# Scaling and rotating each half of the tokens in a quantum of its own, with transposes and scores one quantum later, in the attention layer of a two-layer trunk

## The chip, the core and the metric

The kernel runs on one core of a Trainium2 chip. The metric is device time in microseconds of one execution. The engines are named as in the profile: PE is the matrix engine (PEld its weight loads), DVE the vector engine, ACT the scalar engine, POOL the engine called GpSimd, SP the engine that issues most of the loads. Each engine takes its own instructions in order; between engines there are semaphores.

## What is computed

A trunk of two layers on 256 tokens of 2048 features, all in float32. Layer 0 mixes tokens by block-sparse attention; with 256 tokens there is one block of 256 keys, so it is causal attention with 16 heads of 128. Layer 1 mixes by multi-head latent attention. Each is followed by a gated channel mixer with a short convolution. The change lies in layer 0's attention:

```python
def moba_attention(h, pos, wq, wk, wv, gq, gk, wo):
    ...
    q = rope(rms_norm((h @ wq).reshape(B, S, H, dh), gq), pos, rot)   # rot = 32 of 128
    k = rope(rms_norm((h @ wk).reshape(B, S, H, dh), gk), pos, rot)
    v = (h @ wv).reshape(B, S, H, dh)
    ...
    s_own = jnp.einsum('bqhd,bhkd->bhqk', qc, k_own).astype(F32) * scale
    ...
    return o.reshape(B, S, H * dh) @ wo
```

So every head of q and of k is divided by its root mean square, multiplied by a gain, and has its first 32 numbers rotated by the token's position, before the scores.

## The kernel before

**Products in three parts.** Every weight is split into a high part (`whi`, rounded to the matrix engine's fp32r type) and the rest (`wlo`), and so is every activation. A product is three matmuls: high by high, low weight by high, high weight by low. Weights come in *pieces* of 128 x 512 numbers. `Stream.split` makes the two parts of a piece: ACT casts `whi` (line 104), DVE subtracts to get `wlo` (line 105). The buffers for the parts hold five pieces, so the cast for piece n+5 waits until PE has done with piece n.

**Quanta.** PE's work is a list of quanta, one for each piece, 192 of them for q, k and v of layer 0: four groups of four heads, and in each group 16 quanta for q, 16 for k, 16 for v. A quantum there is six matmuls of 512 columns (`tok_major`, line 235), three for each half of 128 tokens. Around the quanta the program is written out in a fixed order by a loop at its end: before quantum q come the parts of all pieces up to q+3 (after the first 18 quanta), then the matmuls of q, then everything that was attached to q by `at(q, ...)`. Nothing reorders this later: every engine meets its instructions in this order, so a DVE instruction attached to quantum q stands behind the `wlo` of piece q+3 and ahead of the `wlo` of piece q+4.

**Heads.** When the 16 quanta of q (or k) of a group are done, `plan_heads` attaches their further work (`q` is the last of these quanta; for the first group q's work starts 15 quanta later and k's 9 later, since it needs the norm of the tokens):

- `evac` (ACT, lines 372 and 374) copies the products out of PSUM, at q.
- `squares` (DVE, line 379) sums the squares of each head, one half of the tokens at q+1, the other at q+2.
- `rstd` at q+3: DVE writes `hms` (line 387), POOL raises it to the power -1/2 into `hr` (line 392).
- `scaled` (DVE, line 405, four instructions for each half) multiplies by `hr` and the gain, in place in `qk`.
- `rotate` (DVE, lines 435, 436, 439 and 440) rotates the first 32 numbers of the four heads of a half.
- `turned` (PE, line 449) transposes two heads at a time, four transposes; `queries_out` or `keys_out` copies them out of PSUM by two ACT copies and one DVE subtraction.

**Scores.** For each head the class `Head` plans scores and the masked row maximum (`biased`, line 495) at its quantum, exponentials one quantum later, division (`normal`) two later, the transpose of the probabilities (`turn`, `turned`) five later, and the product with the values (`values`, `parted`, lines 553 and 554) eight later. The values of a group are copied out (`evac_parts`, lines 608, 609 and 612) at the last quantum of v.

The latent attention of layer 1 calls `plan_heads` too, with `late` at its default of 0 and no rotation there.

Of the kernel before, what the change touches and what calls it, by code (L numbers as in the profile page):

```python
# [115 lines left out]
def trunk(ctx: ExitStack, tc: tile.TileContext, a, out):  # L116
# [99 lines left out]
    def at(q, f, *args):  # L216
        side.setdefault(q, []).append((f, args))

    def first(q, f, *args):
        ahead.setdefault(q, []).append((f, args))  # L220

    def add(f, *args):
        quanta.append((f, args))
        return len(quanta) - 1
# [26 lines left out]
    def feat_major(state, rhs, k0, k_last, first, t_hi, t_lo, n, half=0):  # L251


        if first and half == 0 and "acc" not in state:
            open_bank(state)
        src = rhs()
        o = state["acc"][:, half * S : (half + 1) * S]
        for k in range(n // P):
            kt = k0 + k
            w_hi, w_lo = t_hi[:, k * P : (k + 1) * P], t_lo[:, k * P : (k + 1) * P]  # L260
            mm(o, w_hi, src[:, kt, :S], start=first and k == 0, stop=False, skip_group_check=True)  # L261
            mm(o, w_hi, src[:, kt, S:], start=False, stop=False, skip_group_check=True)  # L262
            mm(o, w_lo, src[:, kt, :S], start=False, stop=kt == k_last, skip_group_check=True)  # L263
# [358 lines left out]
    def plan_heads(q, hs, key, step, out=None, late=0):  # L622

        at(q, hs.evac)
        for t in range(NT):
            at(q + step * (1 + t), hs.squares, t)
        at(q + step * 3, hs.rstd)
        for t in range(NT):
            at(q + step * (5 + t), hs.scaled, t)
            at(q + step * (5 + t), hs.rotate, t)  # L630
        for i0 in (0, 2):
            pair = {}
            q1 = q + step * 9 + i0 // 2 + late
            at(q1, lambda hs=hs, p=pair, i0=i0, key=key: hs.turned(env[key], p, i0))
            if out is None:
                at(q1, lambda hs=hs, p=pair, i0=i0, key=key: hs.turned_out(env[key], p, i0))
            else:
                at(q1, lambda p=pair, i0=i0, key=key: out(env[key], p["tp"], i0))
# [3 lines left out]
    for g in range(4):  # L642
        for kind in "qkv":
            state = {"first": g == 0 and kind == "q"}
            for kt in range(KD):
                q = add(tok_major, state, lambda: n1.h, kt, KD - 1)
                if g == 0 and kind == "q" and kt + 1 < KD:
                    first(q + 1, n1.scaled, kt + 1)
                if g == 0 and kind == "k" and kt < 12:
                    for j in range(kt * 4 // 3, (kt + 1) * 4 // 3):  # L650
                        at(q, n1.square, j)
                        at(q + 1, n1.total, j)
            if g == 0 and kind == "q":
                at(q + 14, n1.sums)
            if kind == "q":
                at(q, moba_tiles, g)
            if kind == "v":
                at(q, evac_parts, state, ("v", g), lambda: n1.rstd)
                q_v = q
            else:  # L660
                hs = Heads(state, 4, P, G_Q if kind == "q" else G_K, 32, (tab, T_MC, T_MS), lambda: n1.rstd)
                plan_heads(q + (0 if g else 15 if kind == "q" else 9), hs, ("qT" if kind == "q" else "kT", g), 1,
                           queries_out if kind == "q" else keys_out, 1)
                q_k = q
        for i in range(4):
            hd = Head(
                4 * g + i, lambda g=g: env["qT", g], lambda g=g: env["kT", g], lambda g=g: env["v", g],
                i, lambda: env["oT"], MOBA_SCALE, parts=True,
            )
            q0 = q_k + (13 if g else 21) + (2 * i if g == 3 else 3 * i)  # L670
            hd.plan(q0, max(q0 + 8, q_v + 3 + i))


# [260 lines left out]
    for r in range(4):  # L934
        state = {}
        for kq in range(4):
            q = add(lambda t_hi, t_lo, n, st=state, kq=kq: feat_major(
                st, lambda: n3.h, 4 * kq, KD - 1, kq == 0, t_hi, t_lo, n))
# [48 lines left out]
    for half in range(2):  # L987
        state = {}
        for kt in range(KD):
            q = add(tok_major, state, lambda: n3.h, kt, KD - 1)  # L990
# [22 lines left out]
    for g in range(4):  # L1013
        if g == 1:
            rotary_queries(1, 2)
        for kind in "kqv" if g else "qkv":
            state = {}
            for kt in range(4):
                q = add(tok_major, state, lambda kind=kind: env["cqT" if kind == "q" else "ckvT"], kt, 3)
            if kind == ("k" if g else "q"):  # L1020
                at(q, mla_tiles, g)
            if kind == "v":
                at(q, evac_values, state, ("v", g), None)
            else:
                q_q = q
                hs = Heads(state, 4, P, None, 0, None, (lambda: cq["scale"]) if kind == "q" else None,
                           C_GQN if kind == "q" else C_GKN)
                plan_heads(q, hs, ("qT" if kind == "q" else "kT", g), 1)
        for i in range(4):
            hd = Head(  # L1030
                4 * g + i, lambda g=g: env["qT", g], lambda g=g: env["kT", g], lambda g=g: env["v", g],
                i, lambda: env["oT"], MLA_SCALE,
                rope=lambda h=4 * g + i: (env["qrT"][:, h // 2, :], env["kr"][h % 2]),
            )
            q0 = q_q + 11 + 3 * i
            hd.plan(q0, q0 + 7)
# [131 lines left out]
```

## Time and profile before

| | us |
|---|---|
| median of three runs | 2099.79 (2099.70 to 2100.92) |
| the profiled execution | 2099.88 |
| its span in the profile | 2098.0 |
| PE busy in the span | 2089.0 |
| DVE busy in the span | 1405.3 |
| ACT busy in the span | 1138.3 |
| granted PE clock, all slices | full |

The span is what the profiler saw from the first to the last instruction; the rest of the execution's time, 1.88 us, lies around it. Matmuls are pipelined and a matmul's record lasts longer than the interval at which the next can start, so PE's busy share says little of small waits: those are read from the distance between the starts of matmuls.

### The profile page before, as it was taken

Reading aid. Unit: us, or ns where it says so; the run is one execution under the profiler, and the core shown is the slowest. Engines: PE = TensorE matmul, PEld = TensorE weight load, DVE = VectorE, ACT = ScalarE, POOL = GpSimd, SP = SyncE. Lnnn points to the kernel's source line nnn. Section 1 sums busy time; section 2 is a strip of 40 time slices with the busy share of each in tenths; the row PEclk is TensorE's granted clock in tenths of the full one; section 3 lists DMA queues with packets and bytes.
Section 4 is the critical chain, followed back from the end, with each engine's and each line's share of the span. In section 5 each row is a group of like instructions: output and inputs, shape, how many; then the busy total and the mean of one; then the engine's idle time right before and its main releaser. Section 6 shows DMA issues by size and latency. Waiting matters only on the chain.

```text
span 2098.0 us, 42200 instructions
## 1 busy us (share of the span) xinstructions
PE 2089.0 (100%) x16716; PEld 2014.2 (96%) x16716; DVE 1405.3 (67%) x3072; ACT 1138.3 (54%) x2238; POOL 45.6 (2%) x37
## 2 busy tenths in 40 slices
PE   9999999999999999999999999999999999999999
PEld 7888889999999999999999889999999999999999
DVE  6776776776666766655556786766766667655554
ACT  6555555655555555545555675655555555544443
POOL 0000000000000000000000110000000000000000
PEclk9999999999999999999999999999999999999999
DMA  7444445555555555555554533555555555555553
GB/s 272 161 170 173 170 171 185 194 188 198 195 190 200 191 191 201 194 190 198 194 191 159 175 139 108 195 181 201 187 196 199 187 199 195 189 205 209 193 207 131
DMA packets 59382, 391.83 MB, mean 187 GB/s; under 512 B 6960, under 2 KB 10032, under 8 KB 13232
## 3 DMA queue, kind: packets, MB, share of 16 engines
q1 hardware_dynamic: 59040, 388.87, 52.3%
q8 instruction: 131, 2.15, 0.4%
q14 instruction: 67, 0.55, 0.1%
q10 hardware_dynamic: 144, 0.26, 0.0%
HBM read 387.01 MB, written 2.10 MB: 185 GB/s over the span
## 4 chain that ended last, share of the span: by engine, by line
PE 96%; DVE 2%; POOL 0%; ACT 0%; issue 0%; DMA 0%; SPq 0%; ACTq 0%; DVEq 0%; POOLq 0%
PE acc L261 26%; PE acc L263 26%; PE acc L262 26%; PE acc L235 15%; PE tp L449 1%; DVE wlo L105 1%; PE sc L489 0%; PE sc L486 0%; PE tp L521 0%; POOL hr L392 0%; DVE junk L379 0%; PE sc L546 0%; DVE qk L405 0%; DMA xT<-in_xT 0%; PE sc L465 0%
## 5 line engine op out<-in xcount | busy, mean ns | idle before, releaser
L105 DVE TENSOR_TENSOR wlo<-raw,whi 128x512 fp32r<-128x512 f32 (+1 forms) x1480 | 1000.1, 684 | 399.0 <-ACT whi L104 396.0
L104 ACT CAST whi<-raw 128x512 fp32r<-128x512 f32 (+1 forms) x1479 | 871.6, 614 | 459.6 <-PE acc L262 212.3
L261 PE MATMUL acc<-h,whi 128*128 128x256 f32 x2880 | 796.1, 276 | 0.0
L263 PE MATMUL acc<-h,wlo 128*128 128x256 f32 x2880 | 795.9, 276 | 0.0
L262 PE MATMUL acc<-h,whi 128*128 128x256 f32 x2880 | 795.8, 276 | 0.0
L261 PEld LDWEIGHTS acc<-h,whi 128*128 128x128 f32 x2880 | 540.9, 188 | 0.0
L263 PEld LDWEIGHTS acc<-h,wlo 128*128 128x128 f32 x2880 | 540.9, 188 | 0.0
L262 PEld LDWEIGHTS acc<-h,whi 128*128 128x128 f32 x2880 | 540.9, 188 | 0.0
L262 PE MATMUL acc<-a,whi 128*128 128x256 f32 x1408 | 389.1, 276 | 0.0
L263 PE MATMUL acc<-a,wlo 128*128 128x256 f32 x1408 | 389.0, 276 | 0.0
L261 PE MATMUL acc<-a,whi 128*128 128x256 f32 x1408 | 389.0, 276 | 0.0
L235 PE MATMUL acc<-whi,h 128*128 128x512 f32 (+1 forms) x896 | 274.6, 381 | 0.0
L263 PEld LDWEIGHTS acc<-a,wlo 128*128 128x128 f32 x1408 | 264.4, 188 | 0.0
L262 PEld LDWEIGHTS acc<-a,whi 128*128 128x128 f32 x1408 | 264.4, 188 | 0.0
L261 PEld LDWEIGHTS acc<-a,whi 128*128 128x128 f32 x1408 | 264.4, 188 | 0.0
L235 PEld LDWEIGHTS acc<-whi,h 128*128 128x128 f32 x896 | 165.0, 188 | 30.0 <-ACT whi L104 0.7
L235 PE MATMUL acc<-wlo,h 128*128 128x512 f32 (+1 forms) x448 | 170.4, 381 | 2.1 <-DVE wlo L105 2.0
L261 PE MATMUL acc<-oT,whi 128*128 128x256 f32 x512 | 144.9, 283 | 0.0
L263 PE MATMUL acc<-oT,wlo 128*128 128x256 f32 x512 | 141.9, 277 | 0.0
L262 PE MATMUL acc<-oT,whi 128*128 128x256 f32 x512 | 141.7, 277 | 0.0
L740 DVE TENSOR_TENSOR g<-acc,rstd_b 128x256 f32<-128x256 f32 x88 | 37.5, 426 | 125.7 <-PE acc L263 122.7
L747 ACT ACTIVATE c<-g,par 128x256 f32<-128x256 f32 x88 | 53.1, 603 | 108.1 <-DVE g L740 108.1
(160 smaller groups left out, 1603.8 us busy)
## 6 DMA issues: line engine op xcount, KB each, us to landing
raw<-in_ffn_gu SPq DMA_DIRECT2D x176, 1024.0 KB, 4.8
raw<-in_ffn_down SPq DMA_DIRECT2D x88, 1024.0 KB, 4.8
raw<-in_moba_wk SPq DMA_DIRECT2D x16, 1024.0 KB, 4.9
raw<-in_moba_wv SPq DMA_DIRECT2D x16, 1024.0 KB, 4.8
raw<-in_moba_wo SPq DMA_DIRECT2D x16, 1024.0 KB, 4.8
raw<-in_mla_wo SPq DMA_DIRECT2D x16, 1024.0 KB, 4.8
raw<-in_moba_wq SPq DMA_DIRECT2D x13, 1024.0 KB, 4.9
raw<-in_mla_wkv_a SPq DMA_DIRECT2D x8, 576.0 KB, 3.7
```

What stands on the lines that cost most here:

```text
L104: self.nc.scalar.copy(hi[:, :n], w)
L105: self.nc.vector.tensor_tensor(lo[:, :n], w, hi[:, :n].bitcast(F32), op=ALU.subtract)
L235: mm(state["acc"][t][:, :n], src[:, kt, c : c + P], (t_lo if part == 1 else t_hi)[:, :n], start=kt == 0 and part == 0, stop=kt == k_last a ...
L261: mm(o, w_hi, src[:, kt, :S], start=first and k == 0, stop=False, skip_group_check=True)
L262: mm(o, w_hi, src[:, kt, S:], start=False, stop=False, skip_group_check=True)
L263: mm(o, w_lo, src[:, kt, :S], start=False, stop=kt == k_last, skip_group_check=True)
L449: nc.tensor.transpose(tp[:, (i * NT + t) * P : (i * NT + t + 1) * P], flat[:, t, c : c + P], ident)
L740: nc.vector.tensor_tensor(self.g[:, 2:], self.gate["acc"][:, :S], self.norm.rstd_b, op=ALU.mult)
L747: nc.scalar.activation(self.c, self.g[:, 2:], AF.Identity, bias=par[:, cb : cb + 1], scale=self.cw(2))
```

## The change

```diff
@@ plan_heads
         for t in range(NT):
-            at(q + step * (5 + t), hs.scaled, t)
-            at(q + step * (5 + t), hs.rotate, t)
+            at(q + step * (5 + t) + late * (1 + t), hs.scaled, t)
+            at(q + step * (5 + t) + late * (2 + t), hs.rotate, t)
         for i0 in (0, 2):
             pair = {}
-            q1 = q + step * 9 + i0 // 2 + late
+            q1 = q + step * 9 + i0 // 2 + 2 * late
...
@@ heads of layer 0
-            q0 = q_k + (13 if g else 21) + (2 * i if g == 3 else 3 * i)
+            q0 = q_k + (14 if g else 22) + (2 * i if g == 3 else 3 * i)
             hd.plan(q0, max(q0 + 8, q_v + 3 + i))
```

In layer 0 (`step` and `late` both 1), the first half is scaled at q+6 and rotated at q+7, where both stood at q+5; the second half is scaled at q+8 and rotated at q+9, where both stood at q+6. The transposes move from q+10 and q+11 to q+11 and q+12. All work of the heads, from the scores to the product with the values, moves one quantum later: in `max(q0 + 8, q_v + 3 + i)` the first term is the larger for every head, before and after. With `late` at 0, as in layer 1, all these numbers stay as they were. No instruction is added or taken away, and the lists of SP and of POOL keep their order.

## The prediction

> **What bounds the kernel now.** I read the page's busy times first, then the groups by line and form, then the stage of layer 0's q, k and v as a window, then the order of time on PE, DVE, ACT and POOL around each small wait.
>
> ```profile
> span 2098.0 us, 42200 instructions
> PE 2089.0 (100%) x16716; PEld 2014.2 (96%) x16716; DVE 1405.3 (67%) x3072; ACT 1138.3 (54%) x2238; POOL 45.6 (2%) x37
> ```
> ```profile
> L235 PE MATMUL acc<-wlo,h 128*128 128x512 f32 x384 | 151.0, 394 | 2.0 <-DVE wlo L105 2.0
> ```
> ```profile
> 11.60:309.20 297.60, 296.10 (x1449) 246.80 (x1449) 221.17 (x658) 173.29 (x384) 16.89 (x9) 1.00 0.52 185
> ```
>
> PE sets the end: 2089.0 of 2098.0 us, at the full granted clock (the 1.00 of the stage's row). A change on DVE can then only pay where PE waits for DVE. In layer 0's products the second row names such waits: 2.0 us ahead of matmuls with `wlo`. A record ends later than its successor can start, so the true price is in the starts. PE's order of time (start, duration):
>
> ```profile
> 62.43 0.39 PE L235 MATMUL acc<-wlo,h 128*128 128x512 f32 x1
> 62.66 0.61 PE L235 MATMUL acc<-whi,h 128*128 128x512 f32 x2
> 63.60 0.50 PE L235 MATMUL acc<-wlo,h 128*128 128x512 f32 x1 [0.33 <-DVE wlo L105]
> 63.94 0.62 PE L235 MATMUL acc<-whi,h 128*128 128x512 f32 x2
> 64.40 0.40 PE L235 MATMUL acc<-wlo,h 128*128 128x512 f32 x1
> ...
> 64.87 0.60 PE L449 MATMUL tp<-ident,qk 128*128 128x128 f32 x4
> ...
> 77.63 0.39 PE L235 MATMUL acc<-wlo,h 128*128 128x512 f32 x1
> ...
> 79.28 0.50 PE L235 MATMUL acc<-wlo,h 128*128 128x512 f32 x1 [0.81 <-DVE wlo L105]
> ...
> 80.08 0.40 PE L235 MATMUL acc<-wlo,h 128*128 128x512 f32 x1
> ...
> 80.55 0.60 PE L449 MATMUL tp<-ident,qk 128*128 128x128 f32 x4
> ...
> 117.03 0.39 PE L235 MATMUL acc<-wlo,h 128*128 128x512 f32 x1
> ...
> 118.23 0.50 PE L235 MATMUL acc<-wlo,h 128*128 128x512 f32 x1 [0.36 <-DVE wlo L105]
> ...
> 119.03 0.40 PE L235 MATMUL acc<-wlo,h 128*128 128x512 f32 x1
> ...
> 119.50 0.60 PE L449 MATMUL tp<-ident,qk 128*128 128x128 f32 x4
> ...
> 140.39 0.39 PE L235 MATMUL acc<-wlo,h 128*128 128x512 f32 x1
> ...
> 141.14 0.50 PE L235 MATMUL acc<-wlo,h 128*128 128x512 f32 x1
> ...
> 287.67 0.39 PE L235 MATMUL acc<-wlo,h 128*128 128x512 f32 x1
> ...
> 288.40 0.50 PE L235 MATMUL acc<-wlo,h 128*128 128x512 f32 x1
> ```
>
> Undisturbed, a `wlo` matmul follows the last by 0.68 us (62.43, and 63.11 expected): three matmuls, half a quantum, so a quantum is 1.36. The reader is to see 63.60 in place of 63.11, and 0.80 instead of 0.68 to the next: 0.61 lost. At 79.28 it is 0.97 + 0.12 = 1.09, at 118.23 it is 0.52 + 0.12 = 0.64. There is one such place for each of the eight sets of heads (q and k of four groups), always a few matmuls ahead of the first transposes of L449. The other five lie from 141.14 to 288.40 and are near misses: 0.75 - 0.68 = 0.07 at the first, 0.05 at the last, and some 0.11 behind each as at the large ones, 0.16 to 0.18 together. Sum over the stage: 0.61 + 1.09 + 0.64 + 5 x 0.17 = 3.2 us. That is all that DVE costs PE there and all that this change can win.
>
> **Why DVE is late at these places.** The chain at the first, on DVE, with POOL and ACT:
>
> ```profile
> 56.08 1.30 DVE L105 TENSOR_TENSOR wlo<-raw,whi 128x512 fp32r<-128x512 f32 x2
> 58.31 1.14 DVE L405 SCALAR_TENSOR_TENSOR qk<-qk,hr,gains 128x128 f32<-128x128 f32 x4 [0.93 <-POOL hr L392]
> 59.48 0.29 DVE L435 TENSOR_TENSOR ro<-qk,tab 128x128 f32<-128x128 f32 x1
> ...
> 60.29 0.69 DVE L105 TENSOR_TENSOR wlo<-raw,whi 128x512 fp32r<-128x512 f32 x1
> 60.89 1.13 DVE L405 SCALAR_TENSOR_TENSOR qk<-qk,hr,gains 128x128 f32<-128x128 f32 x4
> ```
> ```profile
> 56.26 2.02 POOL L392 TENSOR_TENSOR hr<-hms,mhalf 128x8 f32<-128x8 f32 x1 [5.60 <-DVE hms L387]
> ```
> ```profile
> 56.29 0.62 ACT L104 CAST whi<-raw 128x512 fp32r<-128x512 f32 x1 [0.74 <-PE acc L235]
> 57.65 0.62 ACT L104 CAST whi<-raw 128x512 fp32r<-128x512 f32 x1 [0.74 <-PE acc L235]
> ```
>
> DVE stands still for 0.93 us until POOL's powers land, then scales and rotates the first half (58.31 to 60.29: 1.17 and 0.81), makes one `wlo` (0.60 to the next start), does the second half the same way to 62.87, and only then makes the `wlo` that PE wants at 63.11; it is ready some 0.6 later. The cast that this `wlo` needs was done at 57.65 + 0.62 = 58.27. So it lies 4.6 us behind work that no one wants so soon: the first transposes come at 64.87.
>
> **The change part by part.** Nothing is added or removed; POOL's and SP's instructions keep their order, so no load is issued elsewhere. *Scaling and rotating in four quanta.* Behind the two differences at 56.08 now comes a third (its cast is done at 56.29 + 0.62 = 56.91): 57.38 to 58.0, inside the 0.93 us of idleness. Then, by the durations above and 0.62 for a difference (0.60 from 60.29 to 60.89, rounded up): scaling 58.31 to 59.48, the difference that was late before ready at 60.1, rotation to 60.9, a difference to 61.5, second scaling to 62.7, a difference to 63.3, second rotation to 64.1. The difference wanted at 63.11 has 3.0 us to spare; none later has less than two, since a quantum with scaling takes 1.79 and one with rotation 1.43 against PE's 1.36: four of them fall behind by 1.0 in all. All eight waits go: -3.2 us.
>
> *Transposes one quantum later.* Between the last rotation and the first transposes lay four quanta, now two. At the first place the transposes come at 64.87 - 0.61 + 1.36 = 65.6, against 64.1: 1.5 us to spare. The five small places have the same DVE chain with PE less early, so the same or a little more. Two places are tighter, since other work falls among the halves:
>
> ```profile
> 75.54 0.69 ACT L612 ACTIVATE v<-acc,rstd 128x512 f32<-128x512 f32 x1
> 76.13 1.65 ACT L104 CAST whi<-raw 128x512 fp32r<-128x512 f32 x3
> ```
> ```profile
> 113.57 0.37 ACT L553 CAST oT<-sc 128x256 fp32r<-128x256 f32 x1 [2.58 <-PE sc L544]
> 113.84 1.75 ACT L104 CAST whi<-raw 128x512 fp32r<-128x512 f32 x3
> ```
>
> For k of group 0 the values are copied out in the quantum of the first rotation; the cast behind them ends at 76.13 + 0.62 - 0.61 = 76.1, and then follow on DVE a difference, scaling, a difference, rotation: 3.22 us, to 79.4. The transposes come at 80.55 - 0.61 - 1.09 + 1.36 = 80.2: 0.8 to spare. For q of group 1 the last head's product with the values now falls in the quantum of the first rotation and stands ahead of it on DVE. From the cast at 113.57 to the transposes are 119.50 - 0.64 - 113.57 = 5.3 us, the same number of quanta as after the change; DVE needs from there about 0.4 until it can start line 554 (the cast's 0.37), 0.42 for it (its row below), and 0.81 + 0.62 + 1.17 + 0.62 + 0.81: 4.9. 0.4 to spare. I take 0 for waits of the transposes; the bounds are 0 and, if those two are late by as much as they now have in hand, some 1.2.
>
> *Scores and what follows one quantum later.* The same instructions on the same engines, all shifted together, so their own spacing is kept. New company, for group 0: the division of the last head's probabilities, the copy of the third's transposes and the second's values now meet the first squares of group 1's q.
>
> ```profile
> L379 DVE CUSTOM_DVE_ANT_0 junk<-qk 128x128 f32<-128x128 f32 x128 | 29.6, 289 | 0.0
> L554 DVE TENSOR_TENSOR oT<-sc,oT 128x256 fp32r<-128x256 f32 x32 | 13.6, 424 | 24.0 <-ACT oT L553 24.0
> L513 DVE TENSOR_SCALAR s<-s,sst 128x256 f32<-128x256 f32 x32 | 11.1, 348 | 0.0
> L535 DVE TENSOR_TENSOR pT<-tp,pT 128x256 fp32r<-128x256 f32 x16 | 6.8, 424 | 2.3 <-ACT pT L534 1.7
> ```
>
> On DVE that is 4 x 0.289, twice 0.424, and for the division at most twice 0.348: 2.7 us, with a difference 3.3, so it falls 2.0 behind in a quantum of 1.36, and with the second squares 0.4 more. A difference made as soon as its cast is done has 63.11 - (58.27 + 0.69) = 4.1 us of lead. I take 0; if only half the lead were there, it would cost 0.3. In the last group the work ends a quantum deeper in the output projection, which reads these four heads only from its 25th quantum on; the last values come in its 12th. 0.
>
> One rule speaks against the third difference. The Trainium skill, "SBUF — State Buffer", section "Who interferes with whom", says that a DVE instruction with two SBUF inputs and a GpSimd instruction that reads SBUF shut each other out, the second waiting until the first is done. By that rule the third difference would push the powers, or be pushed, by 0.62 us, and take that from the 1.5 us in hand; the sum would stay within 0.1 of mine but the turn would be nearer. The row at 56.08 speaks against it: its second difference, from 56.7 to 57.4, ran at its usual length inside the powers' 56.26 to 58.28.
>
> **The sum.** The profiled execution took 2099.88 us, 2098.0 of span and 1.88 around it. 2099.88 - 3.2 = 2096.7. It lies 0.09 above the median of 2099.79, so against that median the gain is 3.1, or 0.15%.
>
> **The rivals.** *The transposes take over the waiting (slower).* If the second rotation comes late by x against my tally, PE waits x - 1.5 at six places, x - 0.8 and x - 0.4 at two: 8x - 10.2 in all. From x = 1.7 on this eats the gain; at x = 2.2, about the powers taking twice their 2.02, the sum is 7.4 and the time 2096.7 + 7.4 = 2104.1. For it: the distance is halved, and the tight places are real. Against it: nothing in the chain is new, and 0.93 us of idleness is put to use.
>
> *It doesn't do what it says (same).* If DVE and not the order were short of time, the waits would return on another `wlo`, and the time would stay near 2099.8. For it: DVE is busy 221.17 of 297.60 us in the stage and more around these places. Against it: the late `wlo` had its cast 4.6 us before.
>
> *Half of it.* The three large waits go, but the two tight places turn into waits of 0.5 to 1 each: 2096.7 + 1.6 = 2098.3.
>
> *More than the waits.* If a half quantum behind transposes (0.69 here and there: 119.03 is 0.80 behind 118.23, which I count as refilling) gave back a further 1 to 1.5 us, the time would be 2095.4. Nothing in the rows ties that to DVE.
>
> **How the numbers follow.** Forecast 0.70, at 2096.7; half of it 0.09; unchanged 0.07; transposes take over 0.07; more 0.07. A measurement of this kernel can tell about 0.2% from no change, 4.2 us: below 2095.6 is faster, above 2104.0 slower. All but the last two cases lie within: 0.86, less 0.02 at either edge for runs that differ (2099.70 to 2100.92). Of the slower rival half reaches beyond 4.2 us. Faster 0.09, same 0.86, slower 0.05. The likeliest case alone spans 2096.0 to 2097.8. For eight in ten I reach up to the unchanged case and down to the "more" case: 2095.3 to 2099.8.
>
> **What would show it.** The three `wlo` waits of PE (0.33, 0.81, 0.36) are gone, and that group's idle time falls from 2.0 to about 0.5, what is left being the first two pieces. On DVE three differences stand between `hms` and the first scaling, and the wait for `hr` falls from 0.93 to below 0.35. The end of the q, k, v stage comes 3 us earlier and the latent attention keeps its length. Wrong would be: idle time before L449 waiting for `qk` of L440 or L405, first at k of group 0 and q of group 1; or a later `wlo` with a wait of its own; or a gain that comes from another stage.

## The result and the profile after

| | before | after |
|---|---|---|
| median of 21 runs, us | 2099.92 (2099.29 to 2101.24) | 2096.64 (2096.09 to 2097.58) |
| profiled execution, us | 2099.88 | 2096.73 |
| its span, us | 2098.0 | 2094.9 |

The ratio of the runs is 0.9984, with a 95% interval of 0.9977 to 0.9990, clear of no change: 3.3 us by the medians, where 3.2 was forecast, to 2096.7. The page of the changed kernel, its busy times, and then two of its groups by line and form (busy time, mean; idle time just before them and what ended it):

```profile
span 2094.9 us, 42206 instructions
PE 2086.9 (100%) x16716; PEld 2014.8 (96%) x16716; DVE 1403.5 (67%) x3072; ACT 1137.7 (54%) x2238; POOL 45.6 (2%) x37
```
```profile
L235 PE MATMUL acc<-wlo,h 128*128 128x512 f32 x384 | 150.0, 391 | 0.4 <-DVE wlo L105 0.4
...
L405 DVE SCALAR_TENSOR_TENSOR qk<-qk,hr,gains 128x128 f32<-128x128 f32 x64 | 18.2, 347 | 1.9 <-POOL hr L392 1.9
```

The same instructions, as many on each engine; the six more in the page's total are semaphore events of ACT, which are not counted as busy. The idle time ahead of matmuls with `wlo` fell from 2.0 to 0.4 us, and that of DVE for the powers from 7.4 (0.93 at the first of eight places) to 1.9. Where the time came from is seen in the length of the stage, from the sums of the norm (L326) to the first matmul of the output projection (L261). PE's order of time, before:

```profile
48.79 0.50 PE L326 MATMUL tp<-ones,nacc 128*128 128x1 f32 x4
...
299.95 0.28 PE L261 MATMUL acc<-oT,whi 128*128 128x256 f32 x1
```

and after, with the first transposes between:

```profile
49.00 0.50 PE L326 MATMUL tp<-ones,nacc 128*128 128x1 f32 x4
...
64.00 0.39 PE L235 MATMUL acc<-wlo,h 128*128 128x512 f32 x1
...
64.68 0.39 PE L235 MATMUL acc<-wlo,h 128*128 128x512 f32 x1
...
65.82 0.60 PE L449 MATMUL tp<-ident,qk 128*128 128x128 f32 x4
66.18 0.48 PE L235 MATMUL acc<-whi,h 128*128 128x512 f32 x1
...
296.78 0.28 PE L261 MATMUL acc<-oT,whi 128*128 128x256 f32 x1
```

The stage took 251.16 us before and 247.78 after, 3.38 less. The rest of the span is some 0.2 longer: the stage starts at 49.00 instead of 48.79, behind the first weights. That start differs from run to run, the stage hardly does: in a second trace of the changed kernel, and in those of the three kernels below that differ from it in layer 1 alone, the stage starts at 48.35 to 49.88 and takes 247.76 to 247.78. Its length is therefore a finer measure than the medians, and it stands beside them below. In the latent attention the stretch from the first transposes (L881) to the first scores (L486) kept its length, 27.38 us before and 27.36 after. The `wlo` matmuls ahead of the first transposes now follow each other by 0.68, with no gap. DVE and POOL at the first place, after:

```profile
56.29 1.89 DVE L105 TENSOR_TENSOR wlo<-raw,whi 128x512 fp32r<-128x512 f32 x3
58.51 1.14 DVE L405 SCALAR_TENSOR_TENSOR qk<-qk,hr,gains 128x128 f32<-128x128 f32 x4 [0.32 <-POOL hr L392]
59.56 0.68 DVE L105 TENSOR_TENSOR wlo<-raw,whi 128x512 fp32r<-128x512 f32 x1
60.17 0.28 DVE L435 TENSOR_TENSOR ro<-qk,tab 128x128 f32<-128x128 f32 x1
...
60.97 0.68 DVE L105 TENSOR_TENSOR wlo<-raw,whi 128x512 fp32r<-128x512 f32 x1
61.57 1.13 DVE L405 SCALAR_TENSOR_TENSOR qk<-qk,hr,gains 128x128 f32<-128x128 f32 x4
62.62 0.68 DVE L105 TENSOR_TENSOR wlo<-raw,whi 128x512 fp32r<-128x512 f32 x1
...
63.81 0.29 DVE L440 TENSOR_TENSOR qk<-ro,ro 128x128 f32<-128x128 f32 x1
```
```profile
56.46 2.01 POOL L392 TENSOR_TENSOR hr<-hms,mhalf 128x8 f32<-128x8 f32 x1 [5.60 <-DVE hms L387]
```

Three differences stand where two did, the wait for the powers is 0.32 instead of 0.93, and between any two of the four quanta of scaling and rotating there is a difference. The second rotation ends at 64.10, 1.7 us ahead of the transposes at 65.82.

### The profile page after: what moved, and what is told of

Read it like the earlier page. It is cut to its first block, busy times and chain, and to the rows that moved or that the text cites. A ratio compares the mean times of both kernels' runs of the same rounds, so it can differ in the third digit from the quotient of the medians.

```text
span 2094.9 us, 42206 instructions
## 1 busy us (share of the span) xinstructions
PE 2086.9 (100%) x16716; PEld 2014.8 (96%) x16716; DVE 1403.5 (67%) x3072; ACT 1137.7 (54%) x2238; POOL 45.6 (2%) x37
## 4 chain that ended last, share of the span: by engine, by line
PE 98%; DVE 1%; DMA 0%; SPq 0%; issue 0%; ACT 0%; POOL 0%; POOLq 0%; ACTq 0%
PE acc L261 26%; PE acc L263 26%; PE acc L262 26%; PE acc L235 17%; PE tp L449 1%; PE sc L489 1%; PE tp L521 1%; PE sc L486 0%; PE sc L546 0%; DVE wlo L105 0%; DMA xT<-in_xT 0%; PE sc L465 0%; PE sc L466 0%; PE sc L464 0%; PE sc L544 0%; PE sc L547 0%
## 5 line engine op out<-in xcount | busy, mean ns | idle before, releaser
L261 PE MATMUL acc<-h,whi 128*128 128x256 f32 x2880 | 796.1, 276 | 0.0
L261 PEld LDWEIGHTS acc<-h,whi 128*128 128x128 f32 x2880 | 540.8, 188 | 0.0
L261 PE MATMUL acc<-a,whi 128*128 128x256 f32 x1408 | 389.0, 276 | 0.0
L261 PEld LDWEIGHTS acc<-a,whi 128*128 128x128 f32 x1408 | 264.4, 188 | 0.0
L261 PE MATMUL acc<-oT,whi 128*128 128x256 f32 x512 | 144.9, 283 | 0.0
```

## The experiments

Theory: PE lost its 3.2 us because DVE, which takes its list in order, made a difference too late, behind work that was not needed yet; the remedy is any order that puts the difference ahead, as long as the transposes keep their distance. The rivals ask which part of the change does it, and how much room there is behind it.

**Delay without quanta of their own.**

```diff
-            at(q + step * (5 + t) + late * (1 + t), hs.scaled, t)
-            at(q + step * (5 + t) + late * (2 + t), hs.rotate, t)
+            at(q + step * (5 + t) + late, hs.scaled, t)
+            at(q + step * (5 + t) + late, hs.rotate, t)
```

> The changed kernel, but with rotation in the same quantum as scaling again: both of the first half at q+6, both of the second at q+7; transposes and scores as changed. Theory (the late difference only has to come ahead of the second half, and one quantum of delay does that, since a third difference then fills DVE's wait for the powers): no wait of PE for wlo is left, 2096.6, the same as the changed kernel. Rival (it needs quanta of their own): the eight waits come back in part, each by at least the 1.2 us that scaling and rotating one half takes beyond a quantum, less the lead: 2098 to 2099.9. Seen in the idle time ahead of L235 with wlo: 0.4 by the theory, above 1.0 by the rival.

2096.30 us (2095.87 to 2097.27), ratio 0.9982 (0.9973 to 0.9991). No wait of PE for `wlo` is left from the stage's sums on, which here took 296.33 - 48.57 = 247.76 us, as in the changed kernel (247.78):

```profile
48.57 0.50 PE L326 MATMUL tp<-ones,nacc 128*128 128x1 f32 x4
...
296.33 0.28 PE L261 MATMUL acc<-oT,whi 128*128 128x256 f32 x1
```

The group's idle time is 0.8 us, more than the 0.4 expected, but all of it lies in the first 14 us, at the first weights. So the delay by one quantum suffices, with rotation in the quantum of scaling; the rival falls. The quanta of their own are not needed for the gain.

This kernel keeps the later transposes and scores, and no run tries the delay without them. In its trace the second rotations end 2.47 us (115.75 to 118.22, q of group 1) to 3.10 us ahead of the transposes, more than a quantum of 1.36. By that estimate some 1.1 would be left with the transposes where they were, so a still smaller edit may be enough; that the scores could stay too is not shown.

**Transposes and scores alone.**

```diff
-            at(q + step * (5 + t) + late * (1 + t), hs.scaled, t)
-            at(q + step * (5 + t) + late * (2 + t), hs.rotate, t)
+            at(q + step * (5 + t) + 0, hs.scaled, t)
+            at(q + step * (5 + t) + 0, hs.rotate, t)
```

> Only the second part of the change: scaling and rotating both halves at q+5 and q+6 as before, transposes and scores one quantum later. Theory (the waits come from what stands ahead of the difference on DVE, not from the transposes): the wait at the first set (0.6) and the five near misses (0.17 each) stay; the two large ones that share quanta with other heads' work shrink, since that work has moved: k of group 0 to about 0.5, q of group 1 to about 0. Sum 0.6 + 0.85 + 0.5 = 2.0 above the changed kernel: 2098.6. Rival (the later scores are what wins): 2096.6. Rival (scaling alone wins): 2099.9.

2099.63 us (2098.85 to 2101.47), ratio 0.9999 (0.9990 to 1.0008): next to nothing is won. In its trace PE's large waits are two instead of three, q of group 0 and k of group 0:

```profile
13.88 0.50 PE L235 MATMUL acc<-whi,h 128*128 128x512 f32 x1 [0.98 <-ACT whi L104]
...
65.64 0.50 PE L235 MATMUL acc<-wlo,h 128*128 128x512 f32 x1 [0.32 <-DVE wlo L105]
...
80.80 0.50 PE L235 MATMUL acc<-wlo,h 128*128 128x512 f32 x1 [0.33 <-DVE wlo L105]
```

By the starts these two cost 0.6 each; that of q of group 1 has shrunk to a near miss of 0.22, and the six near misses make 1.1 together: 2.3 in all at these places, where 2.0 was expected. The stage took 301.17 - 50.84 = 250.33 us, 2.55 more than in the changed kernel; the 0.2 between lies in the matmuls behind each place, a few hundredths of a microsecond at each. The median is another 0.4 higher than that. In the profiled run the start explains the rest: its stage begins 1.84 later than the changed kernel's (the row at 13.88 is a wait for the first weights), and 2096.73 + 2.55 + 1.84 = 2101.12 is its time of 2101.13. The other ten runs, of which the lowest four lie at 2098.85 to 2098.98, left no trace, so whether the start explains the 0.4 of the median stays open. That the later scores win is refuted by the time. That they do nothing (2099.9) is nearer to the median than the theory's 2098.6, and only the trace speaks against it: the stage is 0.8 shorter than before the change, since moving transposes and scores makes a near miss of one large wait (0.64 to 0.22) and takes almost half off another (1.09 to 0.60).

**Quanta of their own alone.**

```diff
-            at(q + step * (5 + t) + late * (1 + t), hs.scaled, t)
-            at(q + step * (5 + t) + late * (2 + t), hs.rotate, t)
+            at(q + step * (5 + t) + late * t, hs.scaled, t)
+            at(q + step * (5 + t) + late * (1 + t), hs.rotate, t)
...
-            q1 = q + step * 9 + i0 // 2 + 2 * late
+            q1 = q + step * 9 + i0 // 2 + late
...
-            q0 = q_k + (14 if g else 22) + (2 * i if g == 3 else 3 * i)
+            q0 = q_k + (13 if g else 21) + (2 * i if g == 3 else 3 * i)
```

> Quanta of their own, but with no delay of the first half and transposes and scores where they were before: scaling at q+5 and q+7, rotation at q+6 and q+8, transposes from q+10. Theory: no wait for wlo is left; the distance from the last rotation to the transposes is two quanta as in the changed kernel, but DVE still idles 0.9 for the powers, so k of group 0 waits at its transposes, 0.5 to 1.2, the others next to nothing: 2097.2 to 2098.2. Rival (only the fill of DVE's idle time wins): 2099.9. Rival (the transposes have time in plenty): 2096.6.

2097.49 us (2096.92 to 2098.76), ratio 0.9987 (0.9978 to 0.9996). One wait is left in the stage, at the transposes of k of group 0, for the second rotation:

```profile
80.20 0.27 PE L449 MATMUL tp<-ident,qk 128*128 128x128 f32 x1
81.09 0.55 PE L449 MATMUL tp<-ident,qk 128*128 128x128 f32 x3 [0.62 <-DVE qk L440]
81.39 0.48 PE L235 MATMUL acc<-whi,h 128*128 128x512 f32 x1
```

From the first transpose to the next product are 1.19 us against 0.36 undisturbed (65.82 to 66.18 after): 0.83, the 0.85 by which its median lies above the changed kernel's. The stage took 0.86 longer than the changed kernel's. DVE's idle time for the powers is 7.4 us here, as before the change, and still no difference is late in the stage:

```profile
L405 DVE SCALAR_TENSOR_TENSOR qk<-qk,hr,gains 128x128 f32<-128x128 f32 x64 | 18.2, 347 | 7.4 <-POOL hr L392 7.4
```

Filling that time is one remedy, spreading is another, and neither needs the other.

**Transposes and scores moved back.**

```diff
-            q1 = q + step * 9 + i0 // 2 + 2 * late
+            q1 = q + step * 9 + i0 // 2 + late
...
-            q0 = q_k + (14 if g else 22) + (2 * i if g == 3 else 3 * i)
+            q0 = q_k + (13 if g else 21) + (2 * i if g == 3 else 3 * i)
```

> The changed kernel with transposes and scores one quantum earlier, where they were before: scaling at q+6 and q+8, rotation at q+7 and q+9, transposes from q+10, one quantum behind the last rotation. Theory (margins of 1.5 at six sets, 0.8 and 0.4 at two, less a quantum of 1.36): PE waits 0 at six sets, 0.6 at k of group 0 and 1.0 at q of group 1, with idle time ahead of L449 for qk: 1.6 in all, 2098.2, and up to 2099.7 if my margins are too large by half a microsecond at these two. Rival (the later transposes are not needed): 2096.6. Rival (all eight wait): above 2100.

2098.22 us (2097.83 to 2100.57), ratio 0.9993 (0.9984 to 1.0002). PE waits at the two places named, and nowhere else in the stage:

```profile
78.20 0.27 PE L449 MATMUL tp<-ident,qk 128*128 128x128 f32 x1
79.10 0.55 PE L449 MATMUL tp<-ident,qk 128*128 128x128 f32 x3 [0.62 <-DVE qk L440]
79.40 0.47 PE L235 MATMUL acc<-whi,h 128*128 128x512 f32 x1
...
117.34 0.27 PE L449 MATMUL tp<-ident,qk 128*128 128x128 f32 x1
118.45 0.55 PE L449 MATMUL tp<-ident,qk 128*128 128x128 f32 x3 [0.84 <-DVE qk L440]
118.76 0.48 PE L235 MATMUL acc<-whi,h 128*128 128x512 f32 x1
```

1.20 - 0.36 = 0.84 and 1.42 - 0.36 = 1.06, where 0.6 and 1.0 were expected. The interval of the runs reaches no change, but the stage settles it: 249.71 us, 1.93 longer than the changed kernel's, of the 3.38 that it had won. With the second rotation as late as the changed kernel has it, the transposes have to move too; about half of the gain hangs on that.

**A longer rotation.** Line 435 repeated, its result unchanged, ahead of the second rotation of all eight sets; five times, and in another kernel ten times.

```diff
+                for _ in range(5 if rot == 32 and t == 1 else 0):
+                    nc.vector.tensor_tensor(t1, x[:, :, :rot], over(ct), op=ALU.mult)
                 nc.vector.tensor_tensor(t1, x[:, :, :rot], over(ct), op=ALU.mult)
```

> The changed kernel with five more DVE multiplications (line 435 repeated, its result unchanged) ahead of each second rotation of layer 0, some 1.05 us. It measures the margins of the transposes. Theory (margins 1.5 at six sets, 0.8 at k of group 0, 0.4 at q of group 1): PE waits 0.25 + 0.65 at these two: 2097.5; up to 2098.3 if these margins are nearly used up already. Rival (DVE has room everywhere): 2096.6. Rival (the differences run late first): idle time ahead of L235 with wlo above 0.4.

> The same with ten more multiplications, 2.1 us, ahead of each second rotation. Theory (8x - 10.2 with x = 2.1): six sets wait 0.6, the two tight ones 1.3 and 1.7, 6.6 in all: 2103.2, slower than the kernel before; all of it ahead of L449 for qk, none for wlo. With margins smaller by 0.2 it is 2105. Rival (room everywhere): 2096.6. Rival (only the two tight sets wait): 2099.6.

2098.30 us (2097.97 to 2099.08), ratio 0.9992 (0.9983 to 1.0001), and 2110.13 us (2108.31 to 2112.09), ratio 1.0046 (1.0034 to 1.0059). The second is slower by far more than expected, for two reasons. The first reason, which also puts the kernel with five repeats 0.8 above its 2097.5, is in the added work itself; DVE with five repeats and with ten (start, duration, count):

```profile
63.44 1.59 DVE L436 TENSOR_TENSOR ro<-qk,tab 128x128 f32<-128x128 f32 x5
65.06 0.29 DVE L437 TENSOR_TENSOR ro<-qk,tab 128x128 f32<-128x128 f32 x1
```
```profile
62.84 3.22 DVE L436 TENSOR_TENSOR ro<-qk,tab 128x128 f32<-128x128 f32 x10
66.09 0.29 DVE L437 TENSOR_TENSOR ro<-qk,tab 128x128 f32<-128x128 f32 x1
```

Multiplications that write the same place one after the other start 0.325 us apart (3.25 for ten), not the 0.21 that line 435 and its neighbour show; why is not shown. So x was 1.62 and 3.25 us. PE at three of the eight transposes, with ten repeats:

```profile
65.44 0.27 PE L451 MATMUL tp<-ident,qk 128*128 128x128 f32 x1
67.04 0.55 PE L451 MATMUL tp<-ident,qk 128*128 128x128 f32 x3 [1.33 <-DVE qk L442]
67.34 0.48 PE L235 MATMUL acc<-whi,h 128*128 128x512 f32 x1
...
122.27 0.27 PE L451 MATMUL tp<-ident,qk 128*128 128x128 f32 x1
124.97 0.90 PE L451 MATMUL tp<-ident,qk 128*128 128x128 f32 x3 [2.43 <-DVE qk L442]
125.53 0.78 PE L235 MATMUL acc<-whi,h 128*128 128x512 f32 x1
...
300.12 0.27 PE L451 MATMUL tp<-ident,qk 128*128 128x128 f32 x1
301.31 0.55 PE L451 MATMUL tp<-ident,qk 128*128 128x128 f32 x3 [0.91 <-DVE qk L442]
301.61 0.47 PE L235 MATMUL acc<-whi,h 128*128 128x512 f32 x1
```

Less the 0.36, PE waits 1.54 at the first set, 2.38 at k of group 0, 2.90 at q of group 1 and 1.13 at each of the other five: 12.5 in all. With x = 3.25 the margins of the changed kernel follow: 1.7, 0.9 and 2.1. At q of group 1 the subtraction gives only 0.35, since the clock had fallen by the end of that wait, and the next product came 0.56 behind the transpose of 124.97 instead of 0.30; the changed kernel's own rows give 0.60 there, from the end of the rotation at 118.07 to the transposes at 118.67. Five repeats give 0.86 and 0.60 at the two tight places (they wait 0.76 and 1.02) and no wait at the six others, so these had 1.6 or more. The second reason is PE's clock, told at the end of this document: 1.15 more. 12.5 + 1.15 = 13.6; the stage became 13.7 longer, and 2110.13 - 2096.64 = 13.5. All waits of the stage are at the transposes; in neither kernel is a `wlo` late there.

**The same mechanism in layer 1.** The changed kernel still has a wait of PE for `wlo` there (0.81 us, at 1184.23 of its span):

```profile
1184.23 0.50 PE L235 MATMUL acc<-wlo,cqT 128*128 128x512 f32 x1 [0.81 <-DVE wlo L105]
```

Four edits, one kernel with the first two, one with three, one with all:

```diff
@@ open_room
+        for i in range(2):
+            nc.gpsimd.memset(env["kr"][i], 0.0)
@@ kr_turn, and where it is planned
-            nc.gpsimd.memset(env["kr"][i], 0.0)
...
-    at(q + 9, kr_turn)
+    at(q + 10, kr_turn)
@@ plan_heads, with wait=1 for q of the first group of layer 1 (third edit, then fourth)
-            at(q + step * (5 + t) + late * (1 + t), hs.scaled, t)
+            at(q + step * (5 + t) + late * (1 + t) + wait, hs.scaled, t)
...
-            q1 = q + step * 9 + i0 // 2 + 2 * late
+            q1 = q + step * 9 + i0 // 2 + 2 * late + wait
```

> The changed kernel, and in layer 1 two edits: the two zeroings of the rotary keys by POOL (line 898) are done when their room is opened and no longer behind the powers of the queries' heads, and the transposes of the rotary keys come one quantum later. There the changed kernel still has a wait of PE for wlo (0.81), because DVE waits 1.18 for the zeroing, and one of 0.34 ahead of L894. Theory (the same mechanism as in layer 0: a difference queued on DVE behind a wait that nobody else needs so soon): both go, with 0.1 to 0.2 of refilling: 1.2 to 1.5 us, 2095.2. Rival (the wait comes back behind the powers themselves): 2096.6.

2096.47 us (2095.66 to 2097.58), ratio 0.9982 (0.9973 to 0.9991): the rival held. DVE, rid of the wait for the zeroing, now stands 0.92 us for the powers, and PE waits twice:

```profile
1180.91 0.69 DVE L397 TENSOR_TENSOR qk<-qk,hr 128x512 f32<-128x512 f32 x1 [0.92 <-POOL hr L392]
```
```profile
1183.11 0.50 PE L235 MATMUL acc<-wlo,cqT 128*128 128x512 f32 x1 [0.41 <-DVE wlo L105]
1186.04 0.50 PE L235 MATMUL acc<-wlo,cqT 128*128 128x512 f32 x1 [0.67 <-DVE wlo L105]
```

> The kernel with the two edits in layer 1 (early zeroing of the rotary keys, their transposes one quantum later), and a third: the scaling of q of the first group of layer 1 one quantum later in both halves, transposes where they were. Without the third edit PE still waits 0.41 and 0.67 there for wlo, and DVE 0.92 for the powers. Theory (the same as in layer 0: one quantum later a third difference fills DVE's wait for the powers, and the late differences come ahead): both waits go with some 0.1 of refilling each, 1.3 us: 2095.2, beside 2096.6 of the changed kernel. Rival (the squares of k's heads, which share these quanta, make the differences late whatever the order of the scaling): 2096.4, the waits on another wlo.

> The changed kernel once more, on the same chip as the one before it, so that a difference of one microsecond can be read: 2096.6.

2095.71 us (2095.09 to 2096.92), ratio 0.9981 (0.9972 to 0.9989), beside 2096.71 us (2096.10 to 2097.57) of the changed kernel on the same chip. The two waits are gone, but the transposes took over part of them:

```profile
1185.93 0.55 PE L449 MATMUL tp<-ident,qk 128*128 128x128 f32 x3 [1.11 <-DVE qk L397]
```

> The kernel with the three edits in layer 1, and a fourth: the transposes of q's heads of the first group of layer 1 one quantum later too. Without the fourth edit PE's two waits for wlo there are gone, but it waits 1.11 at these transposes for the second half's scaling (L397). Theory (as in layer 0, delay and turns belong together: the turn has to keep its distance): this wait goes and nothing takes its place, since the scores of this group come five quanta after; 1.0 less than without the edit: 2094.7. Rival (DVE is short of time at this place, and the wait moves on to another wlo or another transpose): 2095.7.

2095.46 us (2094.63 to 2096.72), ratio 0.9980 (0.9971 to 0.9989). That wait is gone, and a smaller one for `wlo` stands in its place:

```profile
1183.88 0.50 PE L235 MATMUL acc<-wlo,cqT 128*128 128x512 f32 x1 [0.38 <-DVE wlo L105]
```

From the first transposes of the compressed keys (L881) to the first scores (L486) the four kernels, in the order changed, two edits, three, four, took 27.36 (1168.40 to 1195.76), 27.10, 26.65 and 25.98 us; a second trace of the changed kernel gives 27.36 again. So by the traces all four edits bring 1.4, and the last one 0.7 of the 1.0 expected, since the wait moved on in part, as its rival said. Of the medians the last, taken on another chip, lies 1.2 us below the changed kernel's and 0.25 below the one ahead of it, with overlapping runs: it is the lowest measured, clearly below the kernel before, and below the changed one by less than the intervals of the runs can settle.

## Why the prediction was right, point by point

*The price of the waits.* The sum over eight places was 3.2 us; the stage became 3.38 shorter and the medians differ by 3.3. The 0.2 that the sum left out is as much as the matmuls behind such places lose in the kernel with later transposes alone. Reading the distance of starts and not the idle time mattered: the idle time fell by only 1.6 us.

*The cause.* That DVE was late by its order and not by its load was right: the same instructions in another order leave no wait. But the prediction gave the four quanta as what removes the waits. The runs show that the delay, with transposes and scores as changed, removes all of them without quanta of their own, and that quanta of their own do so without the delay. The step was not wrong in its numbers, but it did not ask whether one half of the edit was enough. By its own rows it could have: with scaling and rotation together a quantum later, the difference that came 0.49 late would have been made ahead of the second half, 2.6 us earlier.

*The distance of the transposes.* Margins of 1.5, 0.8 and 0.4 us were forecast and 1.7, 0.9 and 0.6 measured; the five others had 2.1, where "the same or a little more" than 1.5 was said. The two tight places were the right two: they are the ones that wait when the transposes are moved back.

*Scores one quantum later at nothing.* Right in the stage after the change. The waits at k of group 0 and at q of group 1 shrink by this move alone, which the prediction did not see; it had counted only new company there, not the company that leaves.

*The rivals.* That the transposes take over the waiting is a true mechanism here: it decides in the kernel with ten repeats, and in layer 1 such a wait of 1.1 us came up. It did not decide in the change, which moves the turns with the scaling. Of the gain "more than the waits" nothing is seen.

*The rule on shared ports.* The Trainium skill, "SBUF — State Buffer", section "Who interferes with whom", would have the third difference and the powers shut each other out. In the changed kernel three differences ran from 56.29 to 58.18 at their usual 0.6 apiece, all but the first 0.17 inside the powers' 56.46 to 58.47, and those took 2.01 us, against 2.02 with two differences before. The measurement decides against the rule for this pair.

## What to carry to other kernels

Where one engine's list holds both the supply of the bound engine and work with time to spare, read for each late supply what stands ahead of it and when that is needed; moving a wait (here for POOL's powers) by one place, so that a supply instruction fills it, costs nothing and may be the whole remedy. Then measure how far ahead of its own consumer the delayed work ends, and move the consumer where that distance is used up: the changed kernel without the later transposes gave back half of the gain, while the delay without quanta of their own left over two microseconds. Price such waits by the distance between starts, not by idle time.

## What the hardware did unexpectedly

In the kernel with ten repeats PE's granted clock fell to half during its longest wait and stayed there for some 3.4 us. The windows of that kernel (stretch and length; busy us of PE, PEld, DVE, ACT and POOL; granted clock; DMA share; GB/s):

```profile
122.00:125.00 3.00, 0.57 (x4) 0.17 (x2) 2.73 (x12) 0.00 (x0) 0.00 (x0) 0.94 0.82 325
125.00:126.50 1.50, 1.50 (x5) 1.34 (x6) 1.12 (x2) 0.59 (x3) 0.00 (x0) 0.50 0.02 5
126.50:128.00 1.50, 1.50 (x5) 1.18 (x4) 1.12 (x2) 0.58 (x2) 0.00 (x0) 0.50 0.00 0
128.00:131.00 3.00, 3.00 (x17) 2.44 (x16) 1.44 (x3) 2.21 (x5) 0.00 (x0) 0.99 0.00 0
```

PE was idle for 2.43 us, from 122.54 to 124.97. The 0.94 of the first row means some 0.36 us at half (0.06 x 3.00 / 0.5), so the clock fell at about 124.6, 2.1 us into the wait, and the column reads 0.50 until 128: the quantum behind took 2.62 us (125.53 to the transposes at 128.15) instead of the 1.47 of an undisturbed one with the same neighbours. An idle time of 2.17 us at k of group 0 in the same kernel left the clock at full speed. The mean granted clock lies below 1.000 in three of the five executions of this kernel (2110.13, 2110.37 and 2112.09 us) and not in the other two (2108.31 and 2109.29), so the fall does not come every time. The Trainium skill, "TensorE: Matmul & The Clock Gate", section "Why this matters for your kernels", asks for no idle gap above some 3 us; in this trace a gap of 2.43 was enough, once.
